# Dates in the written order at three norms, and transposes, evictions and a table load in the attention, of a two-layer trunk

## The chip, the cores and the metric

The kernel runs on one core of a Trainium2 chip. The core has a matrix engine (TensorE, PE in the profile, with its weight loads listed as PEld), a vector engine (VectorE, DVE), a scalar engine (ScalarE, ACT), GpSimd (POOL) and SyncE (SP), which issues most DMAs here. Each engine works through its own list of instructions in order and waits on semaphores for the others. The metric is the device time of one execution in microseconds.

## The reference

Two layers on 256 rows of 2048 numbers, in float32. Every sub-layer is `h = h + RMSNorm(f(RMSNorm(h)))`, with gains of its own in both norms.

```
layer 0:  [xin|C|B] = u @ W_in (2048 x 6144); f = (B * conv3(C * xin)) @ W_out   # causal, depthwise
          MLP: f = square(relu(u @ W_up (2048 x 8192))) @ W_down (8192 x 2048)
then:     K, V = RMSNorm_kv(h) @ W_kv (2048 x 4096)
layer 1:  q = u @ W_q; per head (16 of 128): z = q.k / sqrt(128), strictly causal
          A[t,s] = sigmoid(z[t,s]) * prod_(s<j<t) (1 - sigmoid(z[t,j]));  f = (A V) @ W_o
          MLP as above
```

## The kernel before

**Products.** A float32 operand is split in two: a high part rounded to the engine's fp32r type, and a low part, the rest. A product is three products of parts: high with high, high with low, low with high. The weights come as a stream of 128x1024 tiles in one fixed order. SP loads tile N into `raw` (four buffers, RAW); ACT writes its high part `whiN` (`high_parts`, L146), DVE its low part `wloN` (`low_part`, L157 or, with a gain, L159); the parts have a ring of seven buffers (RING). Tiles 128 and up belong to the up product of the first MLP (135 is its eighth), 384 and up to the kv product (384 to 399 the first half of V, then K and Q), 512 and up to the second MLP.

**Rows and pieces.** The 256 rows are two blocks, b = 0 and 1, and each 2048 wide row is four pieces of 512, c = 0 to 3. Before a product the rows must stand transposed. `enter(b, c)` (L441) has PE transpose piece c of block b into a PSUM bank `tr` (four 128x128 transposes, L208), ACT copy its high part and DVE its low part into `u4` (L214, L215). Together they are called u(b,c) below.

**Groups and units.** `Group` (L240) is a product of the rows with 16 or 8 weight tiles; `unit(b, i)` is the six products of 512 columns (L255 to L257) of block b with tile i. `run` (L276) writes the units, block 0 and 1 alternating. With `enter`, the first EDGE (4) units are written for block 0 in a row and then for block 1. With `leave`, the last four units of each block are written column half by column half, and the norm that follows begins.

**Norms.** `Norms` (L318) ends a sub-layer. As each piece of its product is done, `post` has ACT take the squares' sum and DVE multiply by the gain (`gained`). With the last piece of a block, `finish` forms the root and then the sums h of pieces 0 and 1 (`residual`, L426) and, where there is a gain ahead of the next product, `hg` (`input`, L439). Pieces 2 and 3 follow in two rounds (`round`, L407): the h and hg of both blocks.

**What sets the order at a norm.** Between `begin` and `over` ACT and DVE work in the order in which the code is written, and not in one that a scheduler chooses. That order is a list of dates. `at(delay, fn)` puts a function on a list, and `spent(us)`, called after every unit or product with a planned duration, moves a clock and calls what has come due. TURNS[b][c] are the dates of `enter(b, c)`, counted from the end of block b's last piece for c = 0 and 1 and from block 1's for c = 2 and 3; ROUNDS are the dates of the two rounds. In this stretch a tile's high part is written only as far ahead as `chunk` (up to four tiles, AHEAD) and a limit allow; `allow(n)` raises that limit by n. Low parts are written when `low_parts()` is called at a step, or at the latest when PE's next product wants the tile.

The kernel has three such stretches with a product behind them: the norm after the first output projection (into the first MLP), the norm after the first MLP (into the kv product, no gain ahead, `gpre is None`), and the norm after the attention's output projection (into the second MLP). The first product of an MLP takes six blocks of 128 hidden columns together (LEAD_UP), so that the first eight tiles last while the pieces come in: each block's products of 256 columns (L680), the low parts (L689), then products of 512 columns (L676).

**Attention.** K and Q are made in four groups each, four heads per group, between the two halves of V. `heads_of` (L846) copies a finished product's bank into `tk` on ACT, and 3.0 planned us later PE transposes it into a bank of `abank` (banks 6 and 7 in turn, which `ex`, `ey` and `o` of the heads use as well), from where DVE copies it to `kT` or `qT` (L855). `slots` (L862) dates the heads' steps: scores, logs, weights (`ex` and `ey`, L812 on), and the product with V. `keep_v` (L842) copies a finished value bank to SBUF with a scale, on ACT. `table` (L777) loads one of ACT's function tables at a place in the written order.

Of the kernel before, what the change touches and what calls it, by code (L numbers as in the profile page):

```python
# [34 lines left out]
TURNS = ((3.3, 5.5, 14.0, 19.5), (3.4, 6.0, 10.4, 16.0))  # L35
ROUNDS = (6.4, 11.0)
SQUARES = 20.0
# [24 lines left out]
def trunk(ctx, tc, x, xT, vecs, rows, ws, out):  # L62
# [213 lines left out]
    def run(groups, enter=False, leave=None):  # L276

        units = [(gr, i) for gr in groups for i in range(gr.n)]
        first, last = EDGE if enter else 0, len(units) - (EDGE if leave else 0)
        for b in range(NB):  # L280
            for gr, i in units[:first]:
                gr.unit(b, i)
        for gr, i in units[first:last]:
            if i == 0 and gr.start is not None:
                gr.start()
            for b in range(NB):
                gr.unit(b, i)
        if leave:
            count["limit"] = groups[-1].first + groups[-1].n - 1 + RING - EDGE
            leave.begin()  # L290
            for b in range(NB):
                groups[-1].last_units(b)
# [22 lines left out]
    class Norms:  # L315
# [15 lines left out]
        def post(self, b, c, src, to, scale=None):  # L331

            if (b, c) == (1, 2) and not self.last:
                at(0.69, lambda: self.squared(b, c, src, to, scale))
            else:
                self.squared(b, c, src, to, scale)

        def squared(self, b, c, src, to, scale):
# [9 lines left out]
            if c == 2:  # L348
                t = self.bias[b] = small("bias")
                with tc.high_priority():  # L350
                    nc.vector.tensor_tensor(t[:], self.ss[b][:, 0:1], self.ss[b][:, 1:2], op=ALU.add)
                    nc.vector.tensor_tensor(t[:], t[:], self.ss[b][:, 2:3], op=ALU.add)
                    nc.vector.tensor_scalar(t[:], t[:], 1.0 / D, EPS, op0=ALU.mult, op1=ALU.add)
# [11 lines left out]
        def finish(self, b, gained):  # L365

            with tc.high_priority():
                if b and not self.last:
                    gained()
                    if self.gpre is None:  # L370
                        low_parts()
                r = self.r[b] = inverse_root(self.ss[b][:, 3:4], self.bias[b][:])
# [5 lines left out]
            elif b == 0:  # L378
# [5 lines left out]
                at(TURNS[0][0], lambda: self.input(0, 1))  # L384
# [3 lines left out]
            else:  # L388
                at(0.1, self.second)
                for i in range(2):  # L390
                    at(ROUNDS[i], lambda i=i: self.round(i))
                    for j in range(2):
                        at(TURNS[j][2 + i] - (5.44 if j == 0 else 0.0), lambda i=i, j=j: self.enter(j, 2 + i))
                at(TURNS[1][3] + 0.1, self.over)

        def second(self):

            allow(3 - (self.gpre is None))
            for c in range(2):
                self.residual(1, c)  # L400
                if c == 0:
                    self.input(1, 0)
                at(TURNS[1][c] - 0.1, lambda c=c: self.enter(1, c))
            at(TURNS[1][0] - 0.05, lambda: self.input(1, 1))
            at(TURNS[1][0], lambda: allow(1))

        def round(self, i):  # L407

            low_parts()
            for b in range(NB):  # L410
# [431 lines left out]
    def keep_v(b, c, ps):  # L842
        v[b][c] = result()
        nc.scalar.activation(v[b][c], ps[:], AF.Copy, scale=kv.hs[b][:])

    def heads_of(j, to, scale, then=None):  # L846

        def evict(b, c, ps):
# [5 lines left out]
            def turn():  # L854
                nc.vector.tensor_copy(to[j][:, :, b * P : (b + 1) * P], transposed(t, abank("tr")))  # L855
# [6 lines left out]
    def slots(j):  # L862
# [20 lines left out]
        if j == 3:  # L883
            each(38.5, weights, b)
            at(41.0, lambda: table("sqrt_and_others"))
# [28 lines left out]
    for j in range(4):  # L914
        for i, (name, to, scale) in enumerate((
# [5 lines left out]
            groups.append(Group(W[name, j].base, KD // 2, kv.x4, banks, heads_of(j, to, scale, then), ks=2))  # L921
# [76 lines left out]
```

## Time and profile before

| | us |
|---|---|
| median of three runs | 2192.15 |
| lowest, highest | 2191.85, 2193.22 |
| the profiled execution | 2192.36 |
| its span on the core | 2190.6 |
| PE busy | 2168.5 (99%) |
| DVE busy | 1339.1 (61%) |
| ACT busy | 1130.7 (52%) |

The span runs from the first to the last instruction that the profiler recorded. An engine counts as busy while it executes; the granted clock of PE is 1.00, its upper level, in nearly all of the span. Rows of the trace give a start and a duration in microseconds from the span's start, the engine, the line of the kernel, the operation with what it writes and reads, and in square brackets how long the engine stood idle before and what released it.

### The profile page before, as it was taken

The page shows a single profiled execution, that of the slowest core. Times are in us where ns is not written, and L with a number is a line of the kernel's source. Part 1 is how long each engine was busy: PE and PEld are TensorE (multiplying, and loading weights), DVE is VectorE, ACT ScalarE, POOL GpSimd, SP SyncE. Part 2 cuts the span into 40 slices and gives each one's busy share as a digit, 9 for nine tenths or more (in the row PEclk, how much of TensorE's full clock was granted, in tenths as well). Part 3 has the DMA queues.
Part 4 walks back from the last instruction along what each step waited for, and adds up shares of the span by engine and source line. Part 5 has one row for each costly group of instructions (what it writes and reads, how often), then busy time and mean ns, then how long its engine had stood idle before and what let it go on. Part 6 is the DMA issues. An engine that isn't in the chain of part 4 may idle for free.

```text
span 2190.6 us, 28865 instructions
## 1 busy us (share of the span) xinstructions
PE 2168.5 (99%) x11074; PEld 1853.8 (85%) x11074; DVE 1339.1 (61%) x1830; ACT 1130.7 (52%) x1534; POOL 4.4 (0%) x13
## 2 busy tenths in 40 slices
PE   9999999999999999999999999999999999999998
PEld 8888888888888888888788888888888888888886
DVE  8766656754654664565656777457545645655655
ACT  7544444644543453454467887446445534544543
POOL 0000000000000000000000000000000000000000
PEclk9999999999999999999999999999999999999999
DMA  8655565666566656656565456656665666566663
GB/s 306 205 192 192 188 230 161 210 193 193 190 192 192 193 190 193 194 189 185 165 208 158 162 154 201 186 163 210 192 193 192 190 194 193 188 192 194 187 192 114
DMA packets 114618, 417.18 MB, mean 190 GB/s; under 512 B 12848, under 2 KB 12848, under 8 KB 113456
## 3 DMA queue, kind: packets, MB, share of 16 engines
q1 hardware_dynamic: 112896, 407.95, 59.3%
q0 software_dynamic: 864, 6.29, 0.8%
q8 instruction: 87, 1.43, 0.3%
q10 hardware_dynamic: 720, 1.10, 0.1%
q14 instruction: 51, 0.42, 0.1%
HBM read 413.19 MB, written 2.10 MB: 190 GB/s over the span
## 4 chain that ended last, share of the span: by engine, by line
PE 96%; DVE 2%; ACT 1%; issue 0%; DMA 0%; SPq 0%; DVEq 0%; ACTq 0%
PE up L676 20%; PE acc L255 17%; PE acc L257 17%; PE acc L256 17%; PE up L689 11%; PE acc L538 11%; PE lead L538 1%; PE tr L208 1%; DVE h L426 1%; PE up L680 0%; DVE wlo L157 0%; PE z L785 0%; PE o L833 0%; DMA raw<-w_in 0%; DVE hg L439 0%
## 5 line engine op out<-in xcount | busy, mean ns | idle before, releaser
L157 DVE TENSOR_TENSOR wlo<-raw,whi 128x1024 fp32r<-128x1024 f32 (+1 forms) x678 | 815.7, 1214 | 665.0 <-ACT whi L146 544.5
L146 ACT ACTIVATE whi<-raw 128x1024 fp32r<-128x1024 f32 (+1 forms) x678 | 711.4, 1051 | 648.0 <-PE acc L257 452.1
L676 PE MATMUL up<-u,whi 128*128 128x512 f32 x1952 | 457.9, 390 | 0.0
L676 PEld LDWEIGHTS up<-u,whi 128*128 128x128 f32 x1952 | 361.6, 188 | 71.9
L255 PE MATMUL acc<-whi,hid 128*128 128x512 f32 x1024 | 398.4, 389 | 0.0
L257 PE MATMUL acc<-whi,hid 128*128 128x512 f32 x1024 | 398.3, 389 | 0.0
L256 PE MATMUL acc<-wlo,hid 128*128 128x512 f32 x1024 | 398.3, 389 | 0.0
L689 PEld LDWEIGHTS up<-u,wlo 128*128 128x128 f32 x2048 | 255.8, 191 | 5.8
L689 PE MATMUL up<-u,wlo 128*128 128x256 f32 x2048 | 258.5, 283 | 0.0
L256 PEld LDWEIGHTS acc<-wlo,hid 128*128 128x128 f32 x1024 | 192.2, 188 | 39.9
L257 PEld LDWEIGHTS acc<-whi,hid 128*128 128x128 f32 x1024 | 192.2, 188 | 39.9
L255 PEld LDWEIGHTS acc<-whi,hid 128*128 128x128 f32 x1024 | 192.2, 188 | 39.9
L159 DVE SCALAR_TENSOR_TENSOR wlo<-raw,gv,whi 128x512 fp32r<-128x512 f32 (+1 forms) x160 | 132.1, 853 | 51.2 <-ACT whi L146 50.4
L538 PE MATMUL acc<-u,whi 128*128 128x512 f32 x672 | 156.5, 390 | 0.0
L255 PE MATMUL acc<-whi,u 128*128 128x512 f32 x384 | 153.2, 399 | 0.1
L257 PE MATMUL acc<-whi,u 128*128 128x512 f32 x384 | 149.9, 390 | 0.0
L256 PE MATMUL acc<-wlo,u 128*128 128x512 f32 x384 | 149.7, 390 | 0.0
L146 ACT ACTIVATE whi<-raw,gv 128x512 fp32r<-128x512 f32 (+1 forms) x160 | 122.0, 800 | 50.2 <-PE acc L257 46.9
L538 PEld LDWEIGHTS acc<-u,whi 128*128 128x128 f32 x672 | 124.7, 188 | 25.0
L202 ACT ACTIVATE hid<-s 128x256 fp32r<-128x256 f32 x128 | 52.9, 417 | 106.2 <-DVE s L659 105.9
L656 ACT ACTIVATE half<-up 128x256 f32<-128x256 f32 x128 | 48.3, 383 | 96.5 <-PE up L689 48.7
L257 PEld LDWEIGHTS acc<-whi,u 128*128 128x128 f32 x384 | 72.1, 188 | 15.5
(135 smaller groups left out, 1681.5 us busy)
## 6 DMA issues: line engine op xcount, KB each, us to landing
raw<-w_up SPq DMA_DIRECT2D x256, 512.0 KB, 4.0
raw<-w_dn SPq DMA_DIRECT2D x256, 512.0 KB, 4.1
raw<-w_in SPq DMA_DIRECT2D x94, 512.0 KB, 3.9
raw<-w_out SPq DMA_DIRECT2D x32, 512.0 KB, 4.4
raw<-w_v SPq DMA_DIRECT2D x32, 512.0 KB, 3.8
raw<-w_k SPq DMA_DIRECT2D x32, 512.0 KB, 4.0
raw<-w_q SPq DMA_DIRECT2D x32, 512.0 KB, 4.0
raw<-w_wo SPq DMA_DIRECT2D x32, 512.0 KB, 3.6
```

Of the source, the lines that this page charges most:

```text
L146: rounded = nc.scalar.activation(hi[:, at], raw[i][:, at], AF.Copy, scale=1.0 if gain is None else gain)
L157: nc.vector.tensor_tensor(lo[:, at], t[:, at], hi[:, at].bitcast(F32), op=ALU.subtract)
L159: nc.vector.scalar_tensor_tensor(lo[:, at], t[:, at], gain, hi[:, at].bitcast(F32), op0=ALU.mult, op1=ALU.subtract)
L202: nc.scalar.activation(hi, src, AF.Copy)
L208: nc.tensor.transpose(to[:, j * P : (j + 1) * P], src[:, j * P : (j + 1) * P], ident[:])
L255: nc.tensor.matmul(ps[:], xh, hi[:, a], start=i == 0 and k == 0, stop=False)
L256: nc.tensor.matmul(ps[:], xh, lo[:, a], start=False, stop=False)
L257: nc.tensor.matmul(ps[:], xl, hi[:, a], start=False, stop=i == self.n - 1 and k == self.ks - 1)
L538: nc.tensor.matmul(ps[:, :cols], w, xs[:, :cols], start=k == 0 and part == parts[0], stop=k == KD - 1 and part == parts[1], skip_group_che ...
L656: nc.scalar.activation(half[:], ps[:, T:], AF.Copy)
L676: nc.tensor.matmul(ps, weight(0, k, n), x, start=begin and k == 0, stop=end and k == KD - 1, skip_group_check=end)
L689: nc.tensor.matmul(pss[n][:, :T], weight(1, k, n), x, start=begin and k == 0, stop=end and k == KD - 1, skip_group_check=begin,)
```

## The change

At the MLP norms the dates of the entries and of the rounds are new: the first round 7.2 instead of 6.4 us after block 1's last piece, the second 15.4 instead of 11.0, and block 0's late pieces no longer lose 5.44 from their date. The squares of (1,2) are no longer put off by 0.69. The input of (0,1) is formed with block 1's third piece, and the sum of the squares later, in `add_up`. The sums of squares of h (SQUARES) come 10 instead of 20 us after `over`.

At the kv norm five units of a block follow each other in place of four (KV_EDGE), `second` allows one tile in place of two and enters (1,0) at a date of its own (KV_TURN), and the gain product of the piece (1,3) moves from `finish` to the second round (`later`).

In the attention the keys' and queries' transposes go to the bank that their own product has just left, except the last query group's, which stay with `abank`. Value tiles with an odd column are copied on DVE instead of ACT. The load of the root's table comes 61.0 instead of 41.0 us after the last query group.

```
--- before.py
+++ after.py
@@ -32,9 +32,11 @@
 AHEAD = 4
 CALM = 12
 UNIT = 1.36
-TURNS = ((3.3, 5.5, 14.0, 19.5), (3.4, 6.0, 10.4, 16.0))
-ROUNDS = (6.4, 11.0)
-SQUARES = 20.0
+TURNS = ((4.0, 5.5, 13.8, 19.5), (3.4, 6.0, 14.8, 21.0))
+ROUNDS = (7.2, 15.4)
+KV_TURN = 4.7
+KV_EDGE = 5
+SQUARES = 10.0
 TILE_HIGH = 0.227
 TILE_LOW = 0.12
 FIRST = 2
@@ -276,7 +278,7 @@
     def run(groups, enter=False, leave=None):
 
         units = [(gr, i) for gr in groups for i in range(gr.n)]
-        first, last = EDGE if enter else 0, len(units) - (EDGE if leave else 0)
+        first, last = KV_EDGE if enter else 0, len(units) - (EDGE if leave else 0)
         for b in range(NB):
             for gr, i in units[:first]:
                 gr.unit(b, i)
@@ -330,12 +332,6 @@
 
         def post(self, b, c, src, to, scale=None):
 
-            if (b, c) == (1, 2) and not self.last:
-                at(0.69, lambda: self.squared(b, c, src, to, scale))
-            else:
-                self.squared(b, c, src, to, scale)
-
-        def squared(self, b, c, src, to, scale):
             with tc.high_priority():
                 nc.scalar.activation(
                     self.dump()[:], src, AF.Square, scale=1.0 if scale is None else scale,
@@ -346,11 +342,18 @@
             else:
                 self.gained(b, c, src, to, scale)
             if c == 2:
-                t = self.bias[b] = small("bias")
-                with tc.high_priority():
-                    nc.vector.tensor_tensor(t[:], self.ss[b][:, 0:1], self.ss[b][:, 1:2], op=ALU.add)
-                    nc.vector.tensor_tensor(t[:], t[:], self.ss[b][:, 2:3], op=ALU.add)
-                    nc.vector.tensor_scalar(t[:], t[:], 1.0 / D, EPS, op0=ALU.mult, op1=ALU.add)
+                if b and not self.last:
+                    self.input(0, 1)
+                else:
+                    self.add_up(b)
+
+        def add_up(self, b):
+
+            t = self.bias[b] = small("bias")
+            with tc.high_priority():
+                nc.vector.tensor_tensor(t[:], self.ss[b][:, 0:1], self.ss[b][:, 1:2], op=ALU.add)
+                nc.vector.tensor_tensor(t[:], t[:], self.ss[b][:, 2:3], op=ALU.add)
+                nc.vector.tensor_scalar(t[:], t[:], 1.0 / D, EPS, op0=ALU.mult, op1=ALU.add)
 
         def gained(self, b, c, src, to, scale):
             with tc.high_priority():
@@ -365,10 +368,11 @@
         def finish(self, b, gained):
 
             with tc.high_priority():
-                if b and not self.last:
+                if b and self.gpre is not None:
                     gained()
-                    if self.gpre is None:
-                        low_parts()
+                elif b and not self.last:
+                    self.later = gained
+                    low_parts()
                 r = self.r[b] = inverse_root(self.ss[b][:, 3:4], self.bias[b][:])
             if self.last:
                 for c in range(3):
@@ -381,7 +385,7 @@
                 gained()
                 self.residual(0, 1)
                 at(TURNS[0][0], lambda: self.enter(0, 0))
-                at(TURNS[0][0], lambda: self.input(0, 1))
+                at(TURNS[0][0], lambda: self.add_up(1))
                 if self.gpre is None:
                     at(TURNS[0][0] + 1.5, lambda: allow(1))
                 at(TURNS[0][1], lambda: self.enter(0, 1))
@@ -390,23 +394,33 @@
                 for i in range(2):
                     at(ROUNDS[i], lambda i=i: self.round(i))
                     for j in range(2):
-                        at(TURNS[j][2 + i] - (5.44 if j == 0 else 0.0), lambda i=i, j=j: self.enter(j, 2 + i))
+                        at(TURNS[j][2 + i], lambda i=i, j=j: self.enter(j, 2 + i))
                 at(TURNS[1][3] + 0.1, self.over)
 
         def second(self):
 
-            allow(3 - (self.gpre is None))
-            for c in range(2):
-                self.residual(1, c)
-                if c == 0:
-                    self.input(1, 0)
-                at(TURNS[1][c] - 0.1, lambda c=c: self.enter(1, c))
+            if self.gpre is None:
+                allow(1)
+                self.residual(1, 0)
+                self.input(1, 0)
+                low_parts()
+                self.residual(1, 1)
+                at(KV_TURN - 0.68, lambda: self.enter(1, 0))
+            else:
+                allow(3)
+                self.residual(1, 0)
+                self.input(1, 0)
+                self.residual(1, 1)
+                at(TURNS[1][0] - 0.1, lambda: self.enter(1, 0))
             at(TURNS[1][0] - 0.05, lambda: self.input(1, 1))
             at(TURNS[1][0], lambda: allow(1))
+            at(TURNS[1][1] - 0.1, lambda: self.enter(1, 1))
 
         def round(self, i):
 
             low_parts()
+            if i and self.gpre is None:
+                self.later()
             for b in range(NB):
                 self.residual(b, 2 + i)
                 self.input(b, 2 + i)
@@ -841,9 +855,13 @@
 
     def keep_v(b, c, ps):
         v[b][c] = result()
-        nc.scalar.activation(v[b][c], ps[:], AF.Copy, scale=kv.hs[b][:])
-
-    def heads_of(j, to, scale, then=None):
+        with tc.high_priority():
+            if c % 2 == 0:
+                nc.scalar.activation(v[b][c], ps[:], AF.Copy, scale=kv.hs[b][:])
+            else:
+                nc.vector.tensor_scalar(v[b][c], ps[:], kv.hs[b][:], None, op0=ALU.mult)
+
+    def heads_of(j, to, scale, banks, then=None):
 
         def evict(b, c, ps):
             t = temp([P, 512], "tk", 1)
@@ -852,7 +870,8 @@
                 to[j] = temp([P, 4, T], "kT" if to is kT else "qT", 2 if to is kT else 1)
 
             def turn():
-                nc.vector.tensor_copy(to[j][:, :, b * P : (b + 1) * P], transposed(t, abank("tr")))
+                to_bank = abank("tr") if then and j == 3 else bank(banks[b][0], "tr")
+                nc.vector.tensor_copy(to[j][:, :, b * P : (b + 1) * P], transposed(t, to_bank))
 
             at(3.0, turn)
             if b == 1 and then:
@@ -882,7 +901,7 @@
             each(35.0, mixed, a)
         if j == 3:
             each(38.5, weights, b)
-            at(41.0, lambda: table("sqrt_and_others"))
+            at(61.0, lambda: table("sqrt_and_others"))
             for p in range(NH // 4, NH // 2 - 1):
                 each(46.0 + 3.8 * (p - NH // 4), mixed, p)
             each(57.5, mixed, b)
@@ -918,7 +937,7 @@
             n = 2 * j + i
             banks = [[(2 * n + b) % 4] for b in range(NB)]
             then = (lambda j=j: slots(j)) if name == "q" else None
-            groups.append(Group(W[name, j].base, KD // 2, kv.x4, banks, heads_of(j, to, scale, then), ks=2))
+            groups.append(Group(W[name, j].base, KD // 2, kv.x4, banks, heads_of(j, to, scale, banks, then), ks=2))
     groups[1].start = to_attention
     groups.append(values(1))
     groups += project(W["wo"], o, 2, lambda b, c, ps: held["mix1"].post(b, c, ps[:], result()))
```

ACT's list at the first MLP norm, before: high parts of the weight tiles 134 to 138, and of the pieces u(1,1), u(0,2), u(1,2), u(0,3) (`u4`, in the order of the rows, from the transposes `tr`).

```order
L146 ACTIVATE whi134_3511<-raw134_3346 128x1024
L214 ACTIVATE u4_3442<-tr_3547 128x4x128
L214 ACTIVATE u4_3570<-tr_3571 128x4x128
L146 ACTIVATE whi135_3676<-raw135_3534 128x1024
L214 ACTIVATE u4_3570<-tr_3596 128x4x128
L146 ACTIVATE whi136_3682<-raw136_3543 128x1024
L146 ACTIVATE whi137_3695<-raw137_3579 128x1024
L214 ACTIVATE u4_3643<-tr_3644 128x4x128
L146 ACTIVATE whi138_3709<-raw138_3604 128x1024
```

And in the changed kernel:

```order
L148 ACTIVATE whi134_3511<-raw134_3346 128x1024
L216 ACTIVATE u4_3442<-tr_3535 128x4x128
L216 ACTIVATE u4_3614<-tr_3615 128x4x128
L216 ACTIVATE u4_3614<-tr_3633 128x4x128
L216 ACTIVATE u4_3683<-tr_3684 128x4x128
L148 ACTIVATE whi135_3697<-raw135_3548 128x1024
L148 ACTIVATE whi136_3714<-raw136_3557 128x1024
L148 ACTIVATE whi137_3720<-raw137_3623 128x1024
L216 ACTIVATE u4_3683<-tr_3703 128x4x128
L148 ACTIVATE whi138_3726<-raw138_3641 128x1024
```

The tile 135 stood behind two pieces and stands behind four; the tiles 136 and 137 stand behind it, and the last piece, u(1,3), still follows them.

ACT's list at the kv norm from u(0,0) on, before: `sq` are the squares of (1,2) and of (1,3), `rstd` the root of block 1, 387 to 391 the fourth to eighth value tile; the later `u4` are u(0,1) and u(1,0).

```order
L214 ACTIVATE u4_9329<-tr_9330 128x4x128
L340 ACTIVATE sq_9340,ss_3466<-mg_5031,rstd2_3924 128x512
L146 ACTIVATE whi387_9353<-raw387_9241,gv_78 128x1024
L340 ACTIVATE sq_9360,ss_3466<-mg_5033,rstd2_3924 128x512
L311 ACTIVATE rstd_9366<-ss_3466,bias_9343 128x1
L214 ACTIVATE u4_9369<-tr_9370 128x4x128
L146 ACTIVATE whi388_9377<-raw388_9259,gv_78 128x1024
L146 ACTIVATE whi389_9380<-raw389_9265,gv_78 128x1024
L214 ACTIVATE u4_9329<-tr_9405 128x4x128
L146 ACTIVATE whi390_9412<-raw390_9271,gv_78 128x1024
L146 ACTIVATE whi391_9522<-raw391_9364,gv_78 128x1024
```

And in the changed kernel, where the `u4` behind tile 389 are u(1,0), u(1,1), u(0,2) and u(1,2); the list goes on with u(0,3) and then tile 391:

```order
L216 ACTIVATE u4_9335<-tr_9336 128x4x128
L336 ACTIVATE sq_9357,ss_3466<-mg_5033,rstd2_3840 128x512
L313 ACTIVATE rstd_9359<-ss_3466,bias_9343 128x1
L148 ACTIVATE whi387_9362<-raw387_9241,gv_78 128x1024
L216 ACTIVATE u4_9365<-tr_9366 128x4x128
L148 ACTIVATE whi388_9373<-raw388_9259,gv_78 128x1024
L148 ACTIVATE whi389_9401<-raw389_9265,gv_78 128x1024
L216 ACTIVATE u4_9335<-tr_9404 128x4x128
L216 ACTIVATE u4_9365<-tr_9426 128x4x128
L216 ACTIVATE u4_9470<-tr_9471 128x4x128
L216 ACTIVATE u4_9470<-tr_9484 128x4x128
L148 ACTIVATE whi390_9500<-raw390_9271,gv_78 128x1024
```

The squares of (1,2) now stand ahead of u(0,0), and the root ahead of tile 387. Tile 390 stood right behind u(1,0), with 391 behind it; now three more pieces stand ahead of 390, and a fourth ahead of 391.

DVE's list at the same norm between the low parts of the tiles 389 and 391, before:

```order
L159 SCALAR_TENSOR_TENSOR wlo389_9381<-raw389_9265,gv_78,whi389_9380 128x1024
L215 TENSOR_TENSOR u4_9369<-tr_9437,u4_9369 128x4x128
L215 TENSOR_TENSOR u4_9450<-tr_9451,u4_9450 128x4x128
L159 SCALAR_TENSOR_TENSOR wlo390_9413<-raw390_9271,gv_78,whi390_9412 128x1024
L159 SCALAR_TENSOR_TENSOR wlo391_9523<-raw391_9364,gv_78,whi391_9522 128x1024
```

And in the changed kernel, where `h` are the sums with the residual, and `mg` the gain product that was in `finish`:

```order
L161 SCALAR_TENSOR_TENSOR wlo389_9402<-raw389_9265,gv_78,whi389_9401 128x1024
L440 SCALAR_TENSOR_TENSOR h0_97<-mg_5021,rstd_9310,h0_97 128x512
L440 SCALAR_TENSOR_TENSOR h1_98<-mg_5031,rstd_9359,h1_98 128x512
L217 TENSOR_TENSOR u4_9470<-tr_9471,u4_9470 128x4x128
L217 TENSOR_TENSOR u4_9470<-tr_9484,u4_9470 128x4x128
L363 SCALAR_TENSOR_TENSOR mg_5033<-mg_5033,rstd2_3840,gpost_3463 128x512
L440 SCALAR_TENSOR_TENSOR h0_97<-mg_5023,rstd_9310,h0_97 128x512
L440 SCALAR_TENSOR_TENSOR h1_98<-mg_5033,rstd_9359,h1_98 128x512
L161 SCALAR_TENSOR_TENSOR wlo390_9501<-raw390_9271,gv_78,whi390_9500 128x1024
L217 TENSOR_TENSOR u4_9518<-tr_9519,u4_9518 128x4x128
L161 SCALAR_TENSOR_TENSOR wlo391_9527<-raw391_9378,gv_78,whi391_9526 128x1024
```

Between the low parts of 389 and 390 stood two pieces, u(1,1) and u(0,2); now four sums, two pieces, u(0,2) and u(1,2), and the gain product of (1,3) stand there, and u(0,3) stands ahead of the low part of 391.

## Rows read from the trace of the kernel before

**Rows 1.** Page part 1: each engine's busy us (share), instructions

```profile
PE 2168.5 (99%) x11074; PEld 1853.8 (85%) x11074; DVE 1339.1 (61%) x1830; ACT 1130.7 (52%) x1534; POOL 4.4 (0%) x13
```

**Rows 2.** Waits of PE, whole span: total us, times, longest us

```profile
PE tr L208 <- DVE hg L439: 3.2, 4, 1.4
PE up L680 <- DVE u L215: 3.0, 2, 1.5
...
PE ey L821 <- DVE kT L855: 1.3, 3, 0.4
...
PE acc L255 <- ACT mg L844: 0.8, 1, 0.8
```

**Rows 3.** Timeline of PE, first MLP norm: start, us, engine, line, operation

```profile
372.63 0.96 PE L680 MATMUL up<-u,whi 128*128 128x256 f32 x6
...
375.11 1.34 PE L680 MATMUL up<-u,whi 128*128 128x256 f32 x9 [1.52 <-DVE u L215]
...
378.51 2.08 PE L689 MATMUL up<-u,wlo 128*128 128x256 f32 x16
381.92 0.63 PE L208 MATMUL tr<-ident,hg 128*128 128x128 f32 x4 [1.33 <-DVE hg L439]
```

**Rows 4.** Timeline of ACT, the same norm

```profile
364.47 2.94 ACT L146 ACTIVATE whi<-raw 128x1024 fp32r<-128x1024 f32 x3
...
374.02 1.06 ACT L146 ACTIVATE whi<-raw 128x1024 fp32r<-128x1024 f32 x1 [0.51 <-DMA raw<-w_up]
```

**Rows 5.** Timeline of DVE, the same norm

```profile
375.57 1.21 DVE L157 TENSOR_TENSOR wlo<-raw,whi 128x1024 fp32r<-128x1024 f32 x1
```

**Rows 6.** Timeline of PE, kv norm

```profile
1071.02 0.39 PE L257 MATMUL acc<-whi,hid 128*128 128x512 f32 x1
1071.69 0.66 PE L208 MATMUL tr<-ident,h 128*128 128x128 f32 x4 [0.29 <-DVE h L426]
...
1075.83 0.39 PE L257 MATMUL acc<-whi,u 128*128 128x512 f32 x1
...
1080.55 0.63 PE L208 MATMUL tr<-ident,h 128*128 128x128 f32 x4 [0.91 <-issue]
1080.94 0.48 PE L255 MATMUL acc<-whi,u 128*128 128x512 f32 x1
...
1091.78 0.39 PE L257 MATMUL acc<-whi,u 128*128 128x512 f32 x1
1092.55 0.63 PE L208 MATMUL tr<-ident,h 128*128 128x128 f32 x4 [0.38 <-DVE h L426]
```

**Rows 7.** Timeline of ACT, kv norm

```profile
1073.60 0.72 ACT L340 ACTIVATE sq<-mg,rstd 128x512 f32<-128x512 f32 x1 [0.61 <-DVE mg L733]
...
1074.32 1.14 ACT L146 ACTIVATE whi<-raw,gv 128x1024 fp32r<-128x1024 f32 x1
...
1077.18 0.29 ACT L311 ACTIVATE rstd<-ss,bias 128x1 f32<-128x1 f32 x1
1077.38 0.58 ACT L214 ACTIVATE u<-tr 128x512 fp32r<-128x512 f32 x1
```

**Rows 8.** Timeline of DVE, kv norm

```profile
1073.48 0.68 DVE L215 TENSOR_TENSOR u<-tr,u 128x512 fp32r<-128x512 f32 x1
1074.44 0.75 DVE L360 SCALAR_TENSOR_TENSOR mg<-mg,rstd,gpost 128x512 f32<-128x512 f32 x1 [0.28 <-ACT sq L340]
...
1079.71 1.40 DVE L426 SCALAR_TENSOR_TENSOR h<-mg,rstd,h 128x512 f32<-128x512 f32 x2
...
1082.45 1.28 DVE L159 SCALAR_TENSOR_TENSOR wlo<-raw,gv,whi 128x1024 fp32r<-128x1024 f32 x1
```

**Rows 9.** Windows, kv norm: length, engines' busy us, granted clock, DMA share, GB/s

```profile
1066.00:1112.00 46.00, 44.42 (x210) 36.03 (x209) 36.32 (x57) 30.68 (x53) 0.00 (x0) 1.00 0.52 164
```

## The prediction

> **What bounds the kernel now.** I read the page's busy shares first: TensorE (PE) is busy for 2168.5 of 2190.6 us [rows 1], so a change can only move time where PE stands still. Next the view of who waited for whom, PE alone: its longest waits are few, and each is under 1.6 us [rows 2]. They lie in four places: two MLP norms (one after the output projection of the convolution, one after that of the attention), the kv norm between the two layers, and the attention. So the third view is the timeline of each place, PE beside ACT (ScalarE) and DVE (VectorE). The reader is to see in it how long before its use an operand is made. Everything outside these places runs as before, and I cost it at nothing.
>
> Where a row shows a start, a product of 512 columns takes 0.23 us to the next, one of 256 columns 0.12 (sixteen in 2.08), a group of four transposes 0.39 (1080.55 to 1080.94) [rows 3, 6]. Below, u(b,c) is the transposed piece c of rows b: PE transposes, ACT writes its high part, DVE its low part.
>
> **The two MLP norms: nothing, or a little lost.** Before, u(1,1) had its low part on DVE behind the whole first round, and PE stood from 373.35 (372.63 and six products) to 375.11: 1.76 us. The transpose of (0,3) came before its input was ready: from 380.43 (378.51 and sixteen) to 381.92, 1.49 us [rows 3]. The first transpose waited some 0.2: the four waits for hg are 3.2 us, and the large ones of the two norms take all but 0.4 [rows 2]. With u(1,1) ahead of the first round and the late pieces' dates 5 us later, these go: 3.45 us a norm.
>
> What is late next is the weight tile 135. Its high part now stands on ACT behind u(0,3), whose transpose PE issues shortly before it needs the tile (ACT's order in the section on the change). Count from X, the start of that transpose. PE is ready for the tile after 0.39, four products of 0.12 and two of 0.23: X+1.33. ACT gets the transposes at X+0.66 (0.63 and a hand-over of 0.03), does u(0,3) in 0.5 and the tile in 1.06 [rows 4]: X+2.2. PE waits 0.9. Then it does three products, the transpose of (1,3), one product and two of the low part, and at X+3.75 needs the tile's low part. That stands on DVE behind u(1,3), and u(1,3) on ACT behind tiles 136 and 137: three tiles take 2.94 [rows 4], so ACT is through with them at X+4.1, with u(1,3) at X+4.65. DVE adds 0.6 and the low part's 1.21 [rows 5]: X+6.5. PE waits 2.7. Added 3.6, removed 3.45: +0.15 a norm, +0.3 for both. Before, that high part was made at 374.02, far ahead of its use, and its load was what it waited for [rows 4]; the load now goes out about 2 us later and still lands ahead of ACT's turn, so I cost it at nothing. The sums of squares, now due 10 us earlier, stand on ACT ahead of tile 139, which PE needs several us later: nothing; with that cover gone, one tile's 1.06.
>
> **The kv norm: 7.6 us lost.**
> (a) The first transpose stands three products later and no longer waits: 1071.69 less 1071.25 gives 0.44 back [rows 6].
> (b) But ACT now does the squares at 1073.60 first and is free at 1074.32 [rows 7]; u(0,0)'s low part follows DVE's product at 1074.44, from 1075.10 to 1075.8 [rows 8]. The third value product needs it; its row is 1075.83. So (a) is spent: 0.
> (c) That low part sets DVE's next steps back by 0.6. The root, 1077.18 in its row, comes at 1077.8 and ends at 1078.1. Then ACT takes tile 387 (1.14) ahead of u(0,1) (0.58): 1079.75 [rows 7]. DVE waits for it with the low part (to 1080.4), and h(1,0) behind takes 0.70 [rows 8]: the transpose goes at 1081.1 where it went at 1080.55, +0.55.
> (d) Tile 387's low part follows h: 1.28, to 1082.35. PE, which is after the transpose in the fourth unit, needs it at about 1081.8: +0.55.
> (e) Since five units now come in a row, the fifth follows at once and needs tile 388's low part. DVE reaches it after h (0.66) and u(1,0) (0.6) and ends at 1084.85; PE is there at 1083.73: +1.1.
> (f) The wait for h at the transpose of (0,3), 1092.55 less 1092.01, goes: -0.54 [rows 6].
> (g) One allowance of a tile less makes 390 the last in ACT's queue, behind u(1,2). From that transpose's start Y, PE is ready at Y+0.39+6 x 0.23 = Y+1.77; ACT has the tile at Y+0.66+0.48+1.14 = Y+2.28: +0.5. Its low part stands behind u(1,2), the late product and both h on DVE: Y+1.26+0.6+3 x 0.66+1.28 = Y+5.1, wanted at Y+2.51: +2.6.
> (h) Tile 391 stands behind u(0,3), whose transpose comes right before the tile's first use: ready Z+0.39, made Z+2.28, +1.9; low part Z+3.56, wanted Z+2.51, +1.0.
> Sum: 0.55+0.55+1.1-0.54+0.5+2.6+1.9+1.0 = 7.66, say 7.6. From the ninth unit on a tile's 1.14 on ACT and 1.28 on DVE lie beside 2.7 us of products, and nothing is left behind.
>
> **The attention: 2.2 us won.** Three times ey waited for the transposes' copy out of the bank that it shares, 1.3 us in all; with the transposes in their products' own banks, free since ACT copied them, that goes. Their next users come a product's group later. What is late next is the bank of ex, which DVE reads for the head before: about 0.1 each. At the start of the output projection PE waited 0.8 for value tiles that leave ACT behind a table load [rows 2]; the load goes later, and half of the tiles go to DVE. A copy with a scale out of a bank on DVE isn't in the trace: between 0.68 (u's low part) and 0.75 (product with a scale) [rows 8], I take 0.68, as both read what this one reads; DVE has room beside the products. If it hadn't, one copy is 0.7. I add 0.1 for the restart after each of the four waits and take 0.3 off for ex: 1.3+0.8+0.4-0.3 = 2.2. It can't be over 3.
>
> **The sum.** 0.3+7.6-2.2 = +5.7 us on the profiled execution (2192.36 us, of it 2190.6 span), which lies 0.2 above the median of the runs: 2192.15+5.7 = 2197.8. If each of the ten new waits is off by 0.3 and a few of them together, the sum is off by 1.5: 2196.3 to 2199.4.
>
> **Rivals.**
> 1. Not slower: at the MLP norms tile 135 comes in time. For it: its high part was made 12 us ahead of use before, and nothing but its place in ACT's queue holds it. Against it: that place is behind u(0,3), whose start PE itself sets, so that the distance doesn't depend on how early PE is. Then 7.2 us of waits are not there: 5.7-7.2 = -1.5, 2190.7. It decides from the point where the two waits of a norm add up to under 2.9 instead of 3.6, since the sum then falls under 4.4.
> 2. The banks do not do what the change says: ex or ey waits as long for something else, as DVE's copies and sums stand in its queue in the same order. The wait at the output projection still goes: 5.7+1.4 = +7.1, 2199.3. For it: ex follows ey within 2 us and DVE is what both wait for; against it: the row names the copy as the last to come [rows 2].
> 3. The clock falls. In this norm PE stood for over 1.5 us of 46 before, and the granted clock stayed at 1.00, the upper level, 2.4 GHz [rows 9]. Now it would stand for some 10 us, 2.6 at a time. If the clock fell to the lower level, 1.2 GHz, for the 24 products of the seventh and eighth unit, each would take 0.23 more: +5.5, 2203.3. The Trainium skill has a rule by which waits between groups of products can do this (TensorE: Matmul & The Clock Gate, "HAM oscillation — how this bites in real kernels"); by that rule the trace so far shows nothing, since no wait in it lowered the clock.
>
> **How the numbers follow.** Forecast 0.68, rival 1 0.12, rival 2 0.13, rival 3 0.04; 0.03 is left for a gain that I don't see. A measurement of this kernel tells 0.2%, 4.4 us, from no change: the bound is 2196.5. Of the forecast's 0.68, 0.15 lies under it. Slower: 0.53+0.13+0.04 = 0.70. Same: 0.15 and 0.10 of rival 1, 0.25. Faster: 0.02 of rival 1 and the 0.03, 0.05. The range, 2193.6 to 2200.2, leaves out most of rival 1 and rival 3 and takes in rival 2; the forecast's own is 2196.3 to 2199.4.
>
> **What would show it.** In the profile after, PE's waits for u's low part and for hg at the MLP norms are gone, and products with the tile's high and low part wait there, 0.9 and 2.7 us, for ACT whi and DVE wlo. In the kv norm value products wait four times at the seventh and eighth unit, 6 us in all, for whi and wlo, and twice before, at the fourth and fifth. ey waits no more. The prediction is wrong if PE's products at the kv norm wait under 5 us in all, or if new waits show outside the four places.

## The result

The changed kernel took 2198.26 us (median of nine runs, 2196.84 to 2201.11); the kernel before, beside it, 2192.36 (nine runs, 2191.85 to 2193.22). The ratio is 1.0029, 95% interval [1.0018, 1.0039]: 5.9 us slower, where 5.7 were forecast. The profiled execution took 2198.2 us with a span of 2196.5, 5.9 over that of before. The runs of the changed kernel lie further apart than those of before; what goes with that stands below, under the clock.

Page part 1 of the profile after: PE is busy for 2.4 us more than in [rows 1], of a span 5.9 us longer.

```profile
PE 2170.9 (99%) x11074; PEld 1855.3 (84%) x11074; DVE 1341.0 (61%) x1834; ACT 1127.3 (51%) x1530; POOL 4.4 (0%) x13
```

Who waited for whom after, PE alone (total us, times, longest us). It answers to [rows 2]: hg, u's low part at L680, ey and the value tiles' copy (mg) are gone, and the parts of weight tiles stand in their place.

```profile
PE up L703 <- DVE wlo L159: 4.8, 2, 2.4
PE acc L258 <- DVE wlo L161: 4.3, 4, 2.4
PE acc L257 <- ACT whi L148: 2.1, 2, 1.7
PE up L690 <- ACT whi L148: 1.4, 2, 0.7
PE tr L210 <- issue: 1.3, 1, 1.3
```

The program has 11074 PE instructions before and after. Set side by side by their number, their starts show where the time went; each line is the difference between two points of the program outside the four places:

| stretch | us later after | forecast |
|---|---|---|
| up to the first MLP norm | -0.2 | 0 |
| first MLP norm | +1.3 | +0.15 |
| kv norm | +7.9 | +7.6 |
| attention | -2.9 | -2.2 |
| second MLP norm | -0.2 | +0.15 |

**The MLP norms.** The timeline of PE in the first one, after, which answers to [rows 3]. From 375 to 385 PE doesn't stand; then it waits twice, for tile 135's high part and, ten instructions on, for its low part.

```profile
384.40 0.63 PE L690 MATMUL up<-u,whi 128*128 128x512 f32 x2
385.71 0.95 PE L690 MATMUL up<-u,whi 128*128 128x512 f32 x3 [0.69 <-ACT whi L148]
...
387.18 0.40 PE L703 MATMUL up<-u,wlo 128*128 128x256 f32 x2
389.95 1.22 PE L703 MATMUL up<-u,wlo 128*128 128x256 f32 x4 [2.38 <-DVE wlo L159]
390.97 2.54 PE L690 MATMUL up<-u,whi 128*128 128x512 f32 x6
```

A row's idle time runs from the end of the product before, and products overlap; counted from start to start, less what a product takes to the next, the two waits are 385.71 - 384.40 - 2 x 0.23 = 0.85 and 389.95 - 387.18 - 0.24 = 2.53 us. ACT there, after: idle for 4.57 us until u(0,3) comes, and only then the tiles 135 to 137 and u(1,3).

```profile
384.12 0.60 ACT L216 ACTIVATE u<-tr 128x512 fp32r<-128x512 f32 x1 [4.57 <-PE tr L210]
384.61 2.94 ACT L148 ACTIVATE whi<-raw 128x1024 fp32r<-128x1024 f32 x3
387.45 0.58 ACT L216 ACTIVATE u<-tr 128x512 fp32r<-128x512 f32 x1
```

DVE, after, idle for 2.63 us behind u(0,3), then u(1,3), and tile 135's low part first of four:

```profile
388.07 0.69 DVE L217 TENSOR_TENSOR u<-tr,u 128x512 fp32r<-128x512 f32 x1 [2.63 <-ACT u L216]
388.68 4.62 DVE L159 TENSOR_TENSOR wlo<-raw,whi 128x1024 fp32r<-128x1024 f32 x4
```

Both engines had room for the tile before; nothing but its place held it (the run tile135_early below bears that out). Read in the code, that place follows from the dates: a tile past the limit is written only when PE's next product asks for it, until `over` lifts the limit, and `over` hangs on TURNS[1][3], 5 us later now (16.0 to 21.0). Before, `over` came ahead of tile 135's first product, and what is written behind `over` a scheduler may place: in the list of before whi135_3676 stands ahead of u(0,3) from tr_3644, though its number says that it was written later.

**The clock.** The same four low products and six wide ones in the second MLP norm, after:

```profile
1503.08 0.74 PE L703 MATMUL up<-u,wlo 128*128 128x256 f32 x4 [2.38 <-DVE wlo L159]
1503.66 1.53 PE L690 MATMUL up<-u,whi 128*128 128x512 f32 x6
```

The wait is the same, 2.38 us, but behind it the products took 0.74 and 1.53 us, and in the first norm 1.22 and 2.54. The windows of the first norm, after (length, then each engine's busy time, the granted clock, DMA share, GB/s), show why: behind the wait the granted clock is 0.50, the lower level, 1.2 GHz, until about 393 us.

```profile
387.00:390.00 3.00, 0.62 (x5) 0.38 (x4) 1.93 (x3) 2.97 (x6) 0.00 (x0) 0.95 0.00 0
390.00:391.00 1.00, 1.00 (x5) 1.00 (x6) 1.00 (x2) 0.97 (x4) 0.00 (x0) 0.50 0.07 29
...
392.00:393.00 1.00, 1.00 (x4) 0.81 (x3) 1.00 (x2) 0.97 (x3) 0.00 (x0) 0.50 0.99 336
...
396.00:400.00 4.00, 4.00 (x24) 3.49 (x23) 3.21 (x7) 3.14 (x3) 0.00 (x0) 1.00 0.89 297
```

The cost is 0.48 + 1.01 = 1.5 us. That is the difference between the two norms' +1.3 and -0.2. So rival 3 did happen in this execution, in another place than the one priced, and shorter.

For runs without a profile only the mean granted clock is on record. It takes in the end of the span, where PE is done and every profile shows the lower level. In the twelve profiles of this case a mean of 0.999 (five) goes with no other fall, 0.998 (five) with one or none, 0.997 with two and 0.996 with three. Of the nine runs of the changed kernel the two fastest, 2196.84 and 2196.99, have 0.999; four from 2198.08 to 2198.36 have 0.998; the three slowest, 2199.53 to 2201.11, have 0.996 or 0.997. Where the clock fell in those without a profile isn't known.

**The kv norm.** The waits in PE's timeline there, after; they answer to [rows 6].

```profile
1076.91 0.50 PE L259 MATMUL acc<-whi,u 128*128 128x512 f32 x1 [0.17 <-DVE u L217]
...
1082.15 0.63 PE L210 MATMUL tr<-ident,h 128*128 128x128 f32 x4 [1.32 <-issue]
...
1083.30 0.50 PE L258 MATMUL acc<-wlo,u 128*128 128x512 f32 x1 [0.28 <-DVE wlo L161]
...
1085.75 0.50 PE L258 MATMUL acc<-wlo,u 128*128 128x512 f32 x1 [0.83 <-DVE wlo L161]
...
1098.43 0.50 PE L257 MATMUL acc<-whi,u 128*128 128x512 f32 x1 [0.33 <-ACT whi L148]
1101.30 0.50 PE L258 MATMUL acc<-wlo,u 128*128 128x512 f32 x1 [2.36 <-DVE wlo L161]
...
1106.25 0.50 PE L257 MATMUL acc<-whi,u 128*128 128x512 f32 x1 [1.72 <-ACT whi L148]
1107.57 0.50 PE L258 MATMUL acc<-wlo,u 128*128 128x512 f32 x1 [0.82 <-DVE wlo L161]
```

In this execution the clock stayed at 1.00 here, as the window of [rows 9] shows, after. In the attention no wait is left in the list.

```profile
1066.00:1112.00 46.00, 38.17 (x175) 29.48 (x174) 27.55 (x41) 18.60 (x31) 0.00 (x0) 1.00 0.28 88
```

### The profile page after: what moved, and what is told of

It reads as the page before. It is cut to its first block, busy times and chain, and to the rows that moved or that the text cites. A ratio compares the mean times of both kernels' runs of the same rounds, so it can differ in the third digit from the quotient of the medians.

```text
span 2196.5 us, 28845 instructions
## 1 busy us (share of the span) xinstructions
PE 2170.9 (99%) x11074; PEld 1855.3 (84%) x11074; DVE 1341.0 (61%) x1834; ACT 1127.3 (51%) x1530; POOL 4.4 (0%) x13
## 4 chain that ended last, share of the span: by engine, by line
PE 96%; ACT 2%; DVE 1%; DMA 1%; issue 0%; DVEq 0%; ACTq 0%
PE up L690 20%; PE acc L258 17%; PE acc L259 17%; PE acc L257 17%; PE up L703 11%; PE acc L552 11%; PE lead L552 1%; PE up L694 1%; PE tr L210 1%; ACT whi L148 1%; DVE h L440 0%; PE z L799 0%; PE o L847 0%; DMA raw<-w_in 0%; ACT sq L336 0%
## 5 line engine op out<-in xcount | busy, mean ns | idle before, releaser
L258 PEld LDWEIGHTS acc<-wlo,u 128*128 128x128 f32 x384 | 72.3, 188 | 18.9 <-DVE wlo L161 5.7
```

The source lines that it names most:

```text
L258: nc.tensor.matmul(ps[:], xh, lo[:, a], start=False, stop=False)
```

## The experiments

All times are medians in us. The kernel before, run beside them, took 2192.10 (att_only, mlp_only, kv_only, tile135_early), 2192.11 (banks_only, kv_tiles, kv_edge4, both_ends) and 2192.29 (table_only, values_only). Where the text says that PE's starts gain or lose, the same instructions are compared by their start with those of before, as in the table above.

| run | median (runs) | lowest to highest | ratio to before, 95% |
|---|---|---|---|
| att_only | 2189.59 (11) | 2189.23 to 2190.02 | 0.9987 [0.9979, 0.9996] |
| banks_only | 2190.80 (11) | 2190.14 to 2191.41 | 0.9994 [0.9985, 1.0002] |
| table_only | 2191.18 (11) | 2190.60 to 2192.59 | 0.9995 [0.9986, 1.0003] |
| values_only | 2191.06 (11) | 2190.83 to 2191.42 | 0.9994 [0.9985, 1.0003] |
| mlp_only | 2193.81 (11) | 2193.02 to 2194.89 | 1.0009 [1.0000, 1.0018] |
| kv_only | 2201.26 (5) | 2199.81 to 2203.42 | 1.0043 [1.0030, 1.0055] |
| kv_tiles | 2193.98 (11) | 2193.77 to 2195.14 | 1.0009 [1.0000, 1.0018] |
| kv_edge4 | 2202.92 (5) | 2201.92 to 2203.28 | 1.0047 [1.0035, 1.0060] |
| tile135_early | 2193.76 (11) | 2191.28 to 2194.62 | 1.0005 [0.9997, 1.0014] |
| both_ends | 2182.29 (5) | 2181.68 to 2182.79 | 0.9954 [0.9942, 0.9967] |

**att_only**: of the change's diff, the three edits of the attention, in `keep_v`, `heads_of` and `slots`.

> The kernel before with the attention's part of the change alone (transposes in their products' banks, odd value tiles on VectorE, the later table load). My theory: the three waits of ey and the wait at the start of the output projection go and nothing takes their place; the trace of the changed kernel gave 2.9 us back there, so 2189.5 us, 2.9 under before (my forecast had 2.2: 2190.2). Rival: the banks bring nothing, since ey waits for VectorE in any case; then only the wait of the output projection goes, about 1.1 us, 2191.3.

2.5 us under before: the theory's side, between the forecast's 2.2 and the changed kernel's 2.9. A wait of 0.3 for `tk` has come into the list: a product of the second half of V waits until ACT has copied the last query group's bank. It was 0.14 before, too short for the list, and is 0.14 in the changed kernel too; here a transpose just ahead of it also loses 0.17.

**banks_only**: `heads_of` alone.

```
-                nc.vector.tensor_copy(..., transposed(t, abank("tr")))
+                to_bank = abank("tr") if then and j == 3 else bank(banks[b][0], "tr")
+                nc.vector.tensor_copy(..., transposed(t, to_bank))
```

> The kernel before with the transposes in their products' banks and nothing else of the change. My theory: the three waits of ey go with their restarts, 1.8 us, and the wait of the output projection stays: 2190.3 us. Rival: ey finds VectorE as late as before, and all of the attention's 2.6 us comes from the value tiles and the table load: 2192.1 us.

1.3 us; the interval holds no change, but all eleven runs lie under the lowest of before (2191.85), the waits of ey are gone from the trace, and PE's starts come 0.6 us earlier at each of the three places, and 0.2 of the sum is lost again at `tk`. The forecast had 1.3 us of waits and three restarts of 0.1, less 0.3 for ex: 1.3. The banks did what the change says, and rival 2 falls.

**table_only**:

```
-            at(41.0, lambda: table("sqrt_and_others"))
+            at(61.0, lambda: table("sqrt_and_others"))
```

> The kernel before with the later table load alone. My theory: at the start of the output projection the first product waits for a bank that a value tile's copy on ScalarE has yet to leave, and that copy stands behind the load (1.28 us); with the load later the copy starts 1.3 us earlier and the wait of 0.84 with its restart goes: 1.1 us less than before, 2191.0 us. Rival: four copies on ScalarE are too many in any case (2.42 us); then under 0.5 us is won, 2191.7 or more.

2191.18, 1.1 us less, as the theory has it; the rival's "under 0.5" falls. It is read together with the next run.

**values_only**:

```
-        nc.scalar.activation(v[b][c], ps[:], AF.Copy, scale=kv.hs[b][:])
+        with tc.high_priority():
+            if c % 2 == 0:
+                nc.scalar.activation(v[b][c], ps[:], AF.Copy, scale=kv.hs[b][:])
+            else:
+                nc.vector.tensor_scalar(v[b][c], ps[:], kv.hs[b][:], None, op0=ALU.mult)
```

> The kernel before with the odd value tiles' copies on VectorE alone, the table load where it was. My theory: with two copies fewer, and ahead of the load in ScalarE's list or behind it, the first bank is left in time and the same wait of 0.84 goes: 2191.0 us, so the two edits buy the same microsecond and are worth no more together. Rival: the load still stands ahead of the first copy, which alone decides; then nothing is won, 2192.1 us.

In each of the two traces PE's starts come 1.13 us earlier at that one place, and the wait for mg is gone; the medians say 1.1 and 1.2, near what these runs can tell, and both intervals hold no change. Before, ACT copied the four tiles behind the load (L778):

```profile
1374.08 1.28 ACT L778 ACT_TABLE_LOAD   x1
1375.37 2.42 ACT L844 ACTIVATE mg<-acc,rstd 128x512 f32<-128x512 f32 x4
```

With the odd tiles on DVE, and the load written where it was, the first tile's copy stands ahead of the load (L816), and so frees its bank in time:

```profile
1373.69 0.67 ACT L884 ACTIVATE mg<-acc,rstd 128x512 f32<-128x512 f32 x1
1374.26 0.52 ACT L863 ACTIVATE lb<-lb 128x384 f32<-128x384 f32 x1
1374.79 1.28 ACT L816 ACT_TABLE_LOAD   x1
```

Either edit buys the whole microsecond, since all three edits together gave 2.5 = 1.3 + 1.2. This edit does two things, a priority for the copies and DVE for the odd tiles; which of them moved the first copy was not run apart.

**kv_only**: the edits of KV_EDGE, `later`, `add_up` and `second`, and the new dates, for the kv norm alone.

> The kernel before with the kv norm's part alone (its dates, five units in a row, one tile less allowed, the late product). My theory: value products wait for the parts of tiles 387, 388, 390 and 391 as in the changed kernel, +7.6 to +7.9 us: 2200.1 us, with 390 and 391 the larger share. Rival: the loss in the changed kernel comes with a lower clock or with what the MLP norms before it leave late; alone it would cost under 5 us, under 2197.4.

2199.81 at best, 7.7 over before, as the theory has it; the rival's "under 5" falls. The median lies 1.5 higher: its run is the profiled one, in which the clock fell once, behind the 2.37 us wait for tile 390's low part, and PE's starts lose 9.4 us across the norm where the changed kernel's lose 7.9. The two fastest runs, 2199.81 and 2199.86, have a mean granted clock of 0.999, the other three 0.997 and 0.998. The waits in its trace are those of the changed kernel, 4.3 for wlo, 2.1 for whi and 1.3 at the transpose.

**kv_tiles**: kv_only with two tiles more allowed, between the rounds.

```
+                if self.gpre is None:
+                    at(11.0, lambda: (allow(2), low_parts(1 << 30)))
                 at(TURNS[1][3] + 0.1, self.over)
```

> The run with the kv norm's part alone, and in it two tiles more allowed 11.0 us after block 1's last piece, their low parts written there: the parts of 390 and 391 then stand ahead of u(1,2) and u(0,3). My theory: of the norm's 7.7 us without a fall of the clock, 390's and 391's waits (0.3+2.4+1.7+0.8 us and four restarts of 0.1) go and a wait of 0.7 for h comes back at the transpose of (0,3): 5.0 to 5.5 us less than the lowest executions of that run (2199.8), 2194.5 us, and no execution far above it, as the 2.4 us wait that the clock fell behind is gone. Rival: the early steps (tiles 387 and 388, the transpose of (1,0)) are the larger share; then under 3 us come back, over 2197.

2193.98, 0.5 under the theory's number. All waits in that norm's second half are gone; those of the first half stand as they were:

```profile
1080.71 0.63 PE L212 MATMUL tr<-ident,h 128*128 128x128 f32 x4 [1.27 <-issue]
1081.86 0.50 PE L260 MATMUL acc<-wlo,u 128*128 128x512 f32 x1 [0.29 <-DVE wlo L163]
1084.31 0.50 PE L260 MATMUL acc<-wlo,u 128*128 128x512 f32 x1 [0.78 <-DVE wlo L163]
```

So of the 7.7 us, some 6 hang on two tiles that ACT and DVE wrote too late: 5.8 by the times (2199.81 less 2193.98), 6.1 by PE's starts, which lose 1.8 us across the norm and not 7.9. The wait for h at (0,3) that was to come back did not.

**kv_edge4**: kv_only with KV_EDGE = 4.

> The run with the kv norm's part alone, but four units of a block in a row as before. My theory: only the wait for tile 388's low part goes (0.83 us and its restart), 1.0 us less: 2198.8 us in executions without a fall of the clock, 2.0 to 4 us more with one. Rival: the order of units is what makes the later tiles late; then over 3 us come back, under 2196.8.

Of the waits, only that for tile 388's low part is gone, as expected (wlo 3.5 us in three instead of 4.3 in four). Up to the seventh unit it brought what was expected: there PE's starts have lost 1.07 us less than in kv_only. The time didn't follow: no run is below 2201.92. PE behind the wait for tile 390's low part, in this run:

```profile
1098.77 0.79 PE L260 MATMUL acc<-wlo,u 128*128 128x512 f32 x1 [2.37 <-DVE wlo L163]
1099.37 0.63 PE L261 MATMUL acc<-whi,u 128*128 128x512 f32 x1
1099.79 0.63 PE L259 MATMUL acc<-whi,u 128*128 128x512 f32 x1
```

These products come 0.43 us after each other instead of 0.23, and the granted clock is 0.50 from 1098 to 1104 us, and again at that level for most of 1108 to 1112 (0.55 and 0.59 in windows of 2 us). The two stretches cost some 4.3 us: PE's starts lose 11.2 across the norm, against 7.9 less the 1.07. So the time doesn't show the microsecond that the order of units gave back.

**mlp_only**: the MLP norms' edits alone.

> The kernel before with the two MLP norms' part alone (dates, the sum of the squares later, the early sums of h). My theory: 3.45 us of waits go in each norm and waits of 0.7 and 2.4 us for tile 135's (and 519's) parts with their restarts come in their place: within 0.4 us of before, 2192.4 us, in executions in which the granted clock stays at its upper level. In executions in which it falls after the 2.4 us wait, a norm costs 1.6 us more, as in the changed kernel's profile: 2194.0 with one, 2195.6 with both, and the runs spread over more than 1.5 us. Rival: the clock has no part in it; then the runs lie within 1 us of each other, at 2193.7 if the first norm's 1.3 us loss is the norm's own.

The runs form two groups, six from 2193.02 to 2193.81 with a mean granted clock of 0.998, and five from 2194.47 to 2194.89 with 0.997. They go with the theory's figures for one fall and for two (2194.0, 2195.6) and lie 0.2 to 1.1 under them; none is as low as its 2192.4 without a fall. In its profile (2193.18) the clock fell in the first norm and not in the second: 0.77, 0.50 and 0.88 in the three windows of 2 us from 390 us on, behind the same 2.38 us wait, which ended at 389.71. PE's starts lost 1.35 us across the first norm and gained 0.2 across the second. The rival, no part for the clock, falls; and rival 1 of the prediction (2185.2 here) too.

**tile135_early**: the changed kernel, with tile 135 written behind the second round.

```
+                if self.gpre is not None:
+                    at(15.5, lambda: (allow(1), low_parts(1 << 30)))
                 at(TURNS[1][3] + 0.1, self.over)
```

> The changed kernel with one tile more allowed at the two MLP norms, right behind the second round, and its low part written there, so that tile 135's parts stand ahead of u(0,3) on ScalarE and VectorE. My theory: what is late there is only the tile's place in the written order, so both waits of each norm go and nothing is late next: 3.4 to 3.6 us a norm less, and the clock stays up, another 1.6 us in the executions in which it fell: 2198.3-7.0-1.6 = 2189.7 us, and the runs within 1.5 us of each other. Rival: the next tile or the last piece u(1,3) is late in its place; then under 3 us are won in all, over 2195.3.

The waits of both MLP norms are gone, with nothing late behind them: PE's starts gain 3.7 us against before across the first norm and 3.8 across the second. But the time came 4 us out, 2193.76, no run below 2191.28, and the reason is neither theory's: in the kv norm, whose instructions are those of the changed kernel, the clock fell three times in the profiled execution, the first time here, behind waits of 1.31 and 0.29 us:

```profile
1076.00:1078.00 2.00, 0.86 (x5) 0.58 (x5) 2.00 (x3) 1.93 (x3) 0.00 (x0) 1.00 0.00 0
1078.00:1080.00 2.00, 1.86 (x6) 1.32 (x6) 2.00 (x4) 0.25 (x1) 0.00 (x0) 0.74 0.14 57
1080.00:1082.00 2.00, 1.81 (x4) 1.16 (x4) 0.54 (x1) 0.00 (x0) 0.00 (x0) 0.50 0.74 223
```

PE's starts lost 13 us across that norm, against 7.9 in the changed kernel: the three falls took 5.1 of the 7.5 us that the MLP norms won.

**both_ends**: att_only, with the MLP norms as in tile135_early and the kv norm as before.

> The kernel before with the attention's part, and the MLP norms' part with one tile more allowed behind the second round (as in the run with tile 135 early); the kv norm stays as it was. My theory: 2.6 us from the attention, and 3.45 us of waits with some 0.1 of restart each in either MLP norm: 2192.1-2.6-7.0 = 2182.5 us; with no wait over 1 us left in the norms but the kv norm's 0.9, the granted clock stays up and the runs lie within 1 us. Rival: as in the run with tile 135 early, which came out at 2191.3 to 2194.6 with falls of the clock in the kv norm, the time that the MLP norms win is lost to the clock elsewhere: over 2186.

2182.29, the theory's 2182.5 to 0.2 us, 0.9954 of before [0.9942, 0.9967], faster than both kernels. PE's waits over the whole span:

```profile
PE warm L568 <- DVE v L623: 1.3, 1, 1.3
PE lead L578 <- ACT whi L150: 1.1, 2, 0.8
PE tr L212 <- issue: 0.9, 1, 0.9
PE tr L212 <- DVE h L466: 0.7, 2, 0.4
PE acc L259 <- ACT tk L894: 0.2, 1, 0.2
```

At both MLP norms none is left, and the granted clock stays up there (the first norm's window: PE busy for 40.93 of 41 us):

```profile
355.00:396.00 41.00, 40.93 (x282) 37.74 (x281) 31.33 (x51) 22.09 (x40) 0.53 (x1) 1.00 0.47 148
```

## Why the prediction was right, and where it was not

- **The places and the waits**: right. Counted from start to start, the kv norm's four late waits are 0.50, 2.64, 1.93 and 1.09 us, forecast 0.5, 2.6, 1.9 and 1.0; the two early ones 0.45 and 0.98, forecast 0.55 and 1.1; the transpose of (1,0) waits 0.41 longer than in [rows 6], forecast 0.55; those of the MLP norm 0.85 and 2.53, forecast 0.9 and 2.7. Counting along the order of each engine with durations from the rows was enough, and kv_tiles and tile135_early show that the named place in the order is the cause.
- **(a) and (b) of the kv norm**: (b) was costed as just spending (a), and left some 0.3 from start to start at the third value product. Small.
- **The attention**: the term of 2.2 was mis-sized; att_only has 2.5. The banks' share came out (1.3), with the 0.3 lost at `tk` and not at ex; the output projection's wait was worth 1.1 to 1.2 and not 0.9, since the row's 0.84 runs from the end of the product before: from start to start it is 1.00 (1376.11 - 1374.88 - 0.23), and the restart comes on top. The text named the load and the copies together as what ends that wait; either alone ends it.
- **The MLP norms**: +0.15 each was right to 0.35 us where the clock stayed up (second norm, -0.2).
- **Rival 3** was under-weighted. The prediction held 4 in 100 for a fall of the clock, argued from a norm whose longest wait was 0.91 us [rows 6], and set it against waits of 2.6. In the changed kernel's profile it came in the first MLP norm and cost 1.5 us, not 5.5, as it lasted some three microseconds; by their mean granted clock, two of the nine runs had no fall. In the kv norm, the place that was priced, it cost 1.4 us in the profile of kv_only, 4.3 in kv_edge4 and 5.1 in tile135_early. The Trainium skill (TensorE: Matmul & The Clock Gate, "HAM oscillation — how this bites in real kernels") has the clock fall behind waits between groups of products. The trace agrees, with 0.50 behind the 2.38 us wait; but the waits of that section's example are longer, and here the shorter one was enough in some places and not in others.
- **So the number is closer than the working, and that is luck.** The run of the changed kernel at 2196.84 had a mean granted clock of 0.999, that of its profile 0.998: without a fall the change costs some 4.5 us, 1.2 under the sum. The clock, which the sum held at nothing, put back what the attention and the MLP norms had taken off.

What stays open is what decides whether the clock falls. Eight waits of 2.36 to 2.38 us stand in the five profiles that have them (after, kv_only, mlp_only, kv_edge4, tile135_early), and behind five the clock fell. The kv norm has the same waits in the changed kernel (no fall in the profile), kv_only (one) and tile135_early (three). A run that moves the same norm by single microseconds was not tried.

## What to carry to other kernels

Where PE is busy for 99%, count what stands ahead of each operand in its writer's list, from the start of the last thing that PE itself releases; a tile queued behind a transpose that PE issues just ahead of it is late by a fixed time, however early everything else is. A date that is moved takes with it all that hangs on it: here `over`, five microseconds later, kept two engines idle beside a tile that they had room for. Test the parts of a change alone: this one held 2.5 us of gain, 7.7 of loss, and MLP dates that were worth another 7 with one tile allowed earlier.

## What the runs showed of the hardware

A wait of 2.4 us on TensorE can cost half as much again: behind it the granted clock was 0.50, the lower level, for some three microseconds (after, kv_only, mlp_only) or some seven (kv_edge4, tile135_early), products of 512 columns came 0.43 us after each other instead of 0.23, and a stretch of three cost 1.5 us. Once it fell behind waits of 1.31 and 0.29 us (tile135_early). It doesn't happen behind every such wait: in the changed kernel's profile it came in the first MLP norm and not, behind the same 2.38 us, in the second. The runs of a kernel with such waits lie further apart: 2196.84 to 2201.11 for the changed kernel, 2181.68 to 2182.79 for the one without such waits.
